# Mixing the block steps of two matrix quads in a Trainium2 encoder kernel

## The chip, the cores and the metric

The kernel runs on one core of a Trainium2 chip, as one launch for the whole computation. The core's engines have queues of their own: TensorE (PE in the profile, with its weight loads as PEld), VectorE (DVE), ScalarE (ACT), GpSimd (POOL) and SyncE (SP). SP's queue issues plain transfers, POOL's queue also transfers that add to what lies at their target. The metric is the time of one execution on the device in microseconds, as a median over runs.

## The reference

A trunk of two layers works on x of 512 tokens by 1024 features, in float32. Each layer adds attention with a projection, then a gated feed-forward network (FFN) of 2816 hidden columns:

```python
    for l in range(DEPTH):
        h = rms_norm(x, attn_norm_g[l])
        z = jnp.einsum('bsd,dc->bsc', h, w_in[l])
        ...
        mixed = jax.nn.sigmoid(ga) * ya + jax.nn.sigmoid(gb) * yb
        x = x + jnp.einsum('bsd,de->bse', mixed, w_out[l])
        h = rms_norm(x, ffn_norm_g[l])
        u = jax.nn.silu(jnp.einsum('bsd,df->bsf', h, w_gate[l])) * jnp.einsum('bsd,df->bsf', h, w_up[l])
        x = x + jnp.einsum('bsf,fd->bsd', u, w_down[l])
    return x
```

`rms_norm` divides by the root of the mean square of a token and multiplies by a gain for each feature.

## The kernel before

**Precision.** Each float32 matrix is split in a rounded high part and the low part that is left, and a product is the sum of three matmuls: high by high, high by low, low by high. The high part is a cast on ACT. The low part is either a subtraction on DVE, or it is made "by transfer": ACT writes minus the high part, and a transfer on POOL's queue adds the source to it.

**Quads.** The out projection and most of the FFN are done in quads: a product of two-by-two blocks in which seven block products stand for eight. A block step (`block_step`, numbers m = 1 to 7) is one of the seven and has 24 matmuls of 128x256. Its operands are blocks or sums of blocks. The weights' sums are made by `Quad` (`sums`, `high`, `low`), those of the data by `chain_seven`, both on DVE and ACT. A finished step is read out of its PSUM banks by DVE or ACT, and some results stay in the banks as the start of a later step: `seed` copies, and `plus`, a DVE operation of 128x512, adds one bank's result to the next step's. A step m7 waits for the `plus` behind m6, a step m4 for the one behind m7. In `ORDER` the steps of a quad run 1, 5, 6, 2, 7, 3, 4.

**A layer's second half.** First come the 14 block steps of the two `w_out` quads, q0 and q1 (`OUT_STEPS`: 1 and 5 of either, then the rest of q0, then the rest of q1). `add_x` adds each result to x, which lies in SBUF transposed, as eight tiles of 128 features by 512 tokens. When a pair of tiles is done, `gchunk` multiplies them by the gain and splits them, and squares them for the norm. Then 96 matmuls of 128x512 make the lead, the first 256 columns of gate and up, from data that is not yet divided by the norm's root; `evac_g` and `evac_u` multiply by the root's row on their way out of PSUM. In the midst of the lead stand the `ones` matmuls that sum the squares, the root on DVE (15 tiny operations), and four transposed products that spread it over the partitions (`rstd`). `begin_x` then writes x times gain times root to new tiles `xn`, and `chain_seven` makes the seven operands from them. The five FFN quads follow, each with seven steps of gate and seven of up; the down quad of the quad before runs between them. In quad 0 there is no down quad before it; eight products of the lead with the first 256 rows of `w_down` (steps "t", six matmuls of 128x512 each) stand behind the sixth step and those after it, one behind each in layer 0 and two in layer 1. Quad 0 of gate is `first`: two wide loads on SP bring its weights, and a chain of its own makes the operands as soon as something is ready.

**What sets the order.** The program is recorded by a planner. Operations on weights are queued with due times (`at_pos`) on a clock that counts PE's planned work (`tick`): so many microseconds ahead of the step that needs them (the `LEAD_` and `EARLY` numbers). Operations on data are generators (`spawn`) that the planner advances whenever the modelled engine has come near. Each engine then runs its list in that order. All tiles of SBUF come from two arenas (`arena`), packed by lifetime after a dry run, so which buffer a transfer waits for depends on the whole program. Layer 0 stores x to DRAM (`away`) while its quads run and loads it back before the last down quad; layer 1 keeps x in SBUF and transposes it with PE to the output's layout (`chain_out`).

In the profile nearly all operations carry one line, L346, the helper's. So one goes by engine, operation and shape.

Of the kernel before, what the change touches and what calls it, by code (L numbers as in the profile page):

```python
# [12 lines left out]
F32 = mybir.dt.float32  # L13
# [215 lines left out]
def trunk(ctx: ExitStack, tc: tile.TileContext, a: dict, out: bass.AP, lay: Layout):  # L229
# [208 lines left out]
    def spawn(gen, first=False):  # L438
        chains.insert(0 if first else len(chains), [gen, Need()])
# [55 lines left out]
    MOVED = (1, 2, 4)  # L495
    OUT_EARLY = (6.0, 3.0)
# [32 lines left out]

    DORDER = (1, 5, 6, 3, 7, 4, 2)  # L530
# [29 lines left out]
    OUT_STEPS = [(q, m) for q in range(2) for m in ORDER[:2]] + [(q, m) for q in range(2) for m in ORDER[2:]]  # L560
# [10 lines left out]
    def plan_ffn(l):  # L571
# [3 lines left out]
        down = a["w_down"][l]  # L575
        for step in ffn_steps(l):
            if step[0] == "m":
                _, q, w, m = step
                if m == ORDER[0]:
                    t = total[0]  # L580
# [4 lines left out]
                quads[l, q, w].due(m, total[0] - early)  # L585
                early = max(0.0, early - 1.2)
                total[0] += 24 * 0.12
            elif step[0] == "D":
                _, q, m = step
                if m == DORDER[0]:  # L590
                    f0 = 256 + 512 * q
                    srcs = [down[f0 + 256 * h : f0 + 256 * h + 256] for h in range(2)]
                    early = LEAD_LAST if q == QUADS - 1 else 0.0
                    quads[l, q, "w_down"] = Quad(srcs, total[0] - early, False, turned_quad(l, q))
                quads[l, q, "w_down"].due(m, total[0] - early)
# [75 lines left out]
    class Quad:  # L671
# [3 lines left out]
        def __init__(self, srcs, t, first, turn=False):  # L675
            self.srcs = [x.rearrange("(k p) n -> p k n", p=P) for x in srcs]
            self.first, self.turn = first, turn
            self.shape = [self.srcs[0].shape[1], self.srcs[0].shape[2] // 2]
# [21 lines left out]
        def due(self, m, t):  # L700
            if self.first:
                at_pos(t - LEAD_PREP, lambda: done.add((self, m)))
            else:
                needs = {1: [(1, 1)], 2: [(1, 2)], 3: [(1, 2)], 4: [(2, 2)], 5: [(2, 1), (2, 2)]}.get(m, [])
                lead = LEAD_PREP + (LEAD_MOVE if m in MOVED else LEAD_SUMS)
                for i, x in enumerate(needs):
                    at_pos(t - lead - LEAD_BLOCK - 2.0 * (len(needs) - i - 1), lambda x=x: self.fetch(x))
                if m in MOVED:
                    at_pos(t - lead, lambda: (self.high(m), self.low(m)))
                else:  # L710
                    at_pos(t - lead, lambda: self.sums(m))
                    at_pos(t - LEAD_PREP, lambda: self.high(m))
                    at_pos(t - LEAD_PREP + 1.8, lambda: self.low(m))

        def chain(self):


            for m in ORDER:
# [41 lines left out]
        def low(self, m):  # L760
            src, h = self.parts[m]
            lo = buf(self.shape, F32R)
            if m not in (1, 2) if self.first else m in MOVED:
# [115 lines left out]
    xp = [buf([2, S]) for _ in range(KD // 2)]  # L879
    xT = [xp[k // 2][:, k % 2] for k in range(KD)]  # L880
    away = [dp_.tile([P, 2, S], F32, tag=f"away{i}", name=f"away{i}") for i in range(KD // 2)]

    def new_x(i):
        xp[i] = buf([2, S])
        xT[2 * i : 2 * i + 2] = xp[i][:, 0], xp[i][:, 1]
# [472 lines left out]
    def layer(l):  # L1358
# [227 lines left out]
        def chain_seven(tag, parts, tiles, begin):  # L1586
# [7 lines left out]
            def low(m):  # L1594
                src, h = parts[m]
                yield Need("dve", [h], backlog=XLOG)
                lo = buf([4, 256], F32R)
                V.tensor_tensor(lo, src, h.bitcast(F32), ALU.subtract)
# [76 lines left out]
        def chain_turn():  # L1675
            yield Need(keys=[f"{key}m0"])
            for i in range(KD // 2):
                old = xT[2 * i : 2 * i + 2]
                new_x(i)
                for j in range(2):  # L1680
                    yield Need("act", [old[j]])
                    A.copy(by_columns(xT[2 * i + j]), held(old[j]))
            done.add("turned")

        spawn(chain_seven("m", ms, mt, begin_m))
# [32 lines left out]
        def add_x(q, i, t, src, sign):  # L1718
            at = 2 * q + i
            x = xp[at][:, :, 256 * t : 256 * t + 256]  # L1720
# [9 lines left out]
        for q, m in OUT_STEPS:  # L1730
# [27 lines left out]
        xn = []  # L1758

        def begin_x(h):  # L1760
            if h == 0:
                yield Need(keys=[f"rows{nrm.i}"])
                xn.extend(buf([4, S]) for _ in range(2))
# [6 lines left out]
        spawn(chain_seven("x", xs, xn, begin_x), first=True)  # L1770
# [11 lines left out]
        def evac_u(j, ps):  # L1782
            t = act()
            u[j] = act(F32R), act(F32R)
            yield Need("dve", [ps])
            V.tensor_tensor(t, ps, nrm.rows, ALU.mult)
# [257 lines left out]
```

## Time and profile before

| | |
|---|---|
| runs (three) | 1369.6, 1372.53, 1374.24 us, median 1372.53 us |
| the profiled execution | 1367.72 us, span 1365.9 us |
| granted clock of TensorE, mean | 0.999 |
| DVE, ACT, POOL busy | 77%, 64%, 23% of the span |
| DMA | 241.10 MB, mean 177 GB/s |
| first out step, lead, gate quad 0 of layer 0 | at 301.06, 342.43, 366.49 us |
| the same of layer 1 | at 973.21, 1015.46, 1039.53 us |

Times in the profile's rows count from the start of the span. A row of the timeline is a group of equal instructions that follow each other: start, length, engine, operation, count, and in brackets the idle time before them with what ended it. The last instruction of a group of matmuls ends with some 0.2 us of draining that the next group overlaps.

### The profile page before, as it was taken

How to read it: one execution, taken by the hardware profiler on the slowest of the kernel's cores; microseconds unless marked ns; L12 is line 12 of the kernel's file. 1: busy time of each engine (PE TensorE's matmuls, PEld its weight loads, DVE VectorE, ACT ScalarE, POOL GpSimd, SP SyncE). 2: the span in 40 equal slices, each digit the busy share in tenths (PEclk: the TensorE clock that was granted, in tenths of full speed). 3: DMA queues.
4: the chain of work that ended last, by engine and by line, in shares of the span. 5: the costliest groups of instructions: out<-in, count | busy, mean ns of one | idle time of the engine just before them, and what ended most of it. 6: DMA issues, size and time to landing. Idle time of an engine off the chain costs nothing.

```text
span 1365.9 us, 22021 instructions
## 1 busy us (share of the span) xinstructions
PE 1345.4 (98%) x8268; PEld 1204.3 (88%) x8268; DVE 1050.6 (77%) x1886; ACT 880.5 (64%) x1360; POOL 311.5 (23%) x335
## 2 busy tenths in 40 slices
PE   9999999999999999999999999999999999999998
PEld 7888888889889999999888888888998999899997
DVE  6876878479857697888868667784888586969888
ACT  6477667566766666757446675785766565657572
POOL 5542222321211101011253422322112111111110
PEclk9999999999999999999999999999999999999999
DMA  9997898988787769588989978879779668485883
GB/s 230 201 165 138 148 162 161 199 187 216 164 207 184 164 162 255 106 231 190 221 156 181 162 143 162 156 139 225 160 185 180 150 165 213 113 223 137 228 192 99
DMA packets 194859, 241.10 MB, mean 177 GB/s; under 512 B 27056, under 2 KB 156512, under 8 KB 194752
## 3 DMA queue, kind: packets, MB, share of 16 engines
q0 software_dynamic: 104384, 149.93, 58.1%
q1 hardware_dynamic: 89872, 89.08, 22.2%
q8 instruction: 65, 1.06, 0.3%
q10 hardware_dynamic: 496, 0.67, 0.2%
q14 instruction: 42, 0.34, 0.1%
HBM read 174.63 MB, written 4.19 MB: 131 GB/s over the span
## 4 chain that ended last, share of the span: by engine, by line
PE 72%; DVE 12%; DMA 6%; ACT 6%; issue 4%; SPq 0%; POOL 0%; ACTq 0%; DVEq 0%; POOLq 0%
PE banks L346 72%; DVE arena L346 11%; ACT arena L346 5%; DMA arena<-in_w_gate 4%; DMA arena<-in_w_up 1%; DMA arena<-in_x 1%; ACT L346 0%; SPq L346 0%; DVE banks L346 0%; ACT banks L346 0%; POOL arena L346 0%; ACT warm L346 0%; ACTq L346 0%; DVEq L346 0%; ACT sm L346 0%
## 5 line engine op out<-in xcount | busy, mean ns | idle before, releaser
L346 PE MATMUL banks<-arena 128*128 128x256 f32 (+1 forms) x7694 | 1311.2, 330 | 13.1 <-DVE arena L346 6.1
L346 PEld LDWEIGHTS banks<-arena 128*128 128x128 f32 x7694 | 1140.1, 190 | 142.4 <-ACT arena L346 8.8
L346 ACT CAST arena<-arena 128x1024 fp32r<-128x1024 f32 (+2 forms) x387 | 338.4, 903 | 176.8 <-DVE arena L346 158.2
L346 ACT ACTIVATE arena<-arena 128x1024 fp32r<-128x1024 f32 (+2 forms) x304 | 265.3, 892 | 64.5 <-DMA arena<-in_w_in 21.8
L346 DVE TENSOR_TENSOR arena<-arena,arena 128x1024 fp32r<-128x1024 f32 (+2 forms) x282 | 272.6, 978 | 35.4 <-ACT arena L346 33.4
L346 DVE TENSOR_TENSOR arena<-arena 128x1024 f32<-128x1024 f32 (+4 forms) x280 | 247.6, 897 | 22.5 <-DMA arena<-in_w_gate 18.9
L346 POOL DMA_DIRECT2D arena<-in_w_in x163 | 162.2, 1393 | 311.5 <-ACT arena L346 304.2
L346 POOL DMA_DIRECT2D arena<-arena x106 | 94.2, 888 | 579.7 <-ACT arena L346 347.5
L346 DVE TENSOR_TENSOR arena<-banks,arena 128x512 f32<-128x512 f32 (+4 forms) x234 | 155.5, 669 | 55.5 <-PE banks L346 28.0
L346 DVE TENSOR_TENSOR arena<-arena,banks 128x512 f32<-128x512 f32 (+1 forms) x201 | 135.3, 681 | 73.7 <-PE banks L346 73.6
L346 ACT COPY arena<-banks 128x512 f32<-128x512 f32 (+1 forms) x110 | 63.9, 585 | 72.3 <-PE banks L346 71.0
L346 ACT CAST arena<-banks 128x512 fp32r<-128x512 f32 (+2 forms) x116 | 64.4, 555 | 63.5 <-PE banks L346 62.4
L346 ACT ACTIVATE arena<-arena,negm 128x256 f32<-128x256 f32 (+1 forms) x128 | 68.2, 533 | 18.6 <-DVE negm L346 16.4
L346 PE MATMUL banks<-cst,arena 128*128 128x128 f32 x504 | 76.9, 274 | 1.9 <-DMA arena<-in_x 1.7
L346 PEld LDWEIGHTS banks<-cst,arena 128*128 128x128 f32 x504 | 61.5, 141 | 11.7 <-DMA arena<-in_x 2.3
L346 DVE CUSTOM_DVE_ANT_0 arena<-banks,cst,nsnk 128x256 f32<-128x256 f32 (+1 forms) x64 | 34.5, 548 | 34.1 <-PE banks L346 33.5
L346 DVE CUSTOM_DVE_ANT_0 arena<-banks,arena 128x256 f32<-128x256 f32 x64 | 26.4, 421 | 21.1 <-PE banks L346 20.8
L346 ACT ACTIVATE arena<-banks 128x512 f32<-128x512 f32 x30 | 18.0, 599 | 31.6 <-PE banks L346 31.6
L346 DVE SCALAR_TENSOR_TENSOR arena<-arena 128x512 f32<-128x512 f32 (+2 forms) x44 | 32.1, 731 | 0.6
L346 DVE TENSOR_TENSOR banks<-banks,arena 128x512 f32<-128x512 f32 x24 | 16.7, 696 | 18.4 <-PE banks L346 18.4
L346 DVE TENSOR_SCALAR arena<-arena,sm 128x256 f32<-128x256 f32 (+1 forms) x88 | 29.7, 389 | 1.1
L346 POOL DMA_DIRECT2D arena<-in_w_proj_b x16 | 17.5, 1289 | 47.7 <-ACT arena L346 47.7
(70 smaller groups left out, 351.9 us busy)
## 6 DMA issues: line engine op xcount, KB each, us to landing
arena<-arena POOLq DMA_DIRECT2D x106, 512.0 KB, 7.3
arena<-in_w_in POOLq DMA_DIRECT2D x99, 512.0 KB, 7.2
arena<-in_w_up SPq DMA_DIRECT2D x40, 512.0 KB
arena<-in_w_down SPq DMA_DIRECT2D x40, 512.0 KB
arena<-in_w_gate SPq DMA_DIRECT2D x36, 512.0 KB
arena<-in_w_in POOLq DMA_DIRECT2D x64, 256.0 KB, 6.6
arena<-in_w_proj_a POOLq DMA_DIRECT2D x16, 512.0 KB, 7.7
arena<-in_w_proj_b POOLq DMA_DIRECT2D x16, 512.0 KB, 7.4
```

The source lines that it names most:

```text
L346: f(*args, **kw)
```

## The change

The order of the 14 steps becomes `MIXED`, a table of (quad, m), for the two `w_out` quads and for gate and up of FFN quad 0, whose steps ran one matrix after the other before. The eight leading down products follow all 14 steps. Gate's quad 0 no longer is `first`: its blocks are fetched one by one and its operands have due times, 12 us early. For `w_out` the low part of m7 is now made by transfer too, and all its due times move ahead. `begin_x` scales x in place. So both layers store x to `away`, and layer 1 loads it again (`back`) at the seventh and eighth step of quad 0; the output's transposes may begin with the eleventh step instead of the third. `evac_g` and `evac_u` first copy the bank to SBUF on ACT, and DVE multiplies there. `chain_seven` makes the operand of m2 ahead of that of m6.

On PE in layer 0, before (the rows are matmuls by shape; the 336 are the 14 out steps, then the lead with `ones` and `rstd`, then quad 0 with its down products):

```order
L346 MATMUL banks<-arena_72 128x256 x336
L346 MATMUL banks<-arena_72 128x512 x45
L346 MATMUL banks<-ones,arena_71 128x1 x4
L346 MATMUL banks<-arena_72 128x512 x18
L346 MATMUL banks<-cst,rstd_3321 128x128 x4
L346 MATMUL banks<-arena_72 128x512 x33
L346 MATMUL banks<-arena_72 128x256 x144
L346 MATMUL banks<-arena_72 128x512 x6
L346 MATMUL banks<-arena_72 128x256 x24
```

and in the changed kernel:

```order
L346 MATMUL banks<-arena_72 128x256 x336
L346 MATMUL banks<-arena_72 128x512 x30
L346 MATMUL banks<-ones,arena_71 128x1 x4
L346 MATMUL banks<-arena_72 128x512 x18
L346 MATMUL banks<-cst,rstd_3302 128x128 x4
L346 MATMUL banks<-arena_72 128x512 x48
L346 MATMUL banks<-arena_72 128x256 x336
L346 MATMUL banks<-arena_72 128x512 x48
```

The `ones` stand 15 matmuls earlier in the lead, and the down products stand in one piece behind 336 matmuls instead of in pieces of six behind the sixth step and those after it.

On DVE at gate's quad 0 in layer 0. In both kernels a copy of the spread root (COPY, 128x512), four `begin_x` scalings (SCALAR_TENSOR_TENSOR with `vec2T`, 128x512) and a sum of 128x1024 stand ahead. Before, from the next row on to `plus` for gate's m7, which is the last row (the 1024-wide rows, also written 4x256, are sums, and with two sources low parts; 512-wide ones with `banks` first among the sources read PSUM):

```order
L346 TENSOR_TENSOR arena0_71<-arena0_71 128x4x256
L346 TENSOR_TENSOR arena1_72<-arena0_71,arena1_72 128x1024 x2
L346 SCALAR_TENSOR_TENSOR arena0_71<-arena0_71,vec2T_78 128x512 x4
L346 SCALAR_TENSOR_TENSOR arena0_71<-arena0_71 128x1024
L346 TENSOR_TENSOR arena0_71<-banks_73,arena0_71 128x512 x2
L346 TENSOR_TENSOR arena1_72<-arena0_71,arena1_72 128x1024 x2
L346 TENSOR_TENSOR arena0_71<-arena0_71 128x4x256
L346 TENSOR_TENSOR arena0_71<-banks_73,arena0_71 128x512
L346 TENSOR_TENSOR arena0_71<-arena0_71 128x512
L346 TENSOR_TENSOR arena1_72<-arena0_71,arena1_72 128x1024 x2
L346 SCALAR_TENSOR_TENSOR arena0_71<-arena0_71 128x1024
L346 TENSOR_TENSOR banks_73<-banks_73,arena0_71 128x512
```

In the changed kernel, up to the same `plus`; between the sum of 128x1024 named above and these rows stand two low parts, four scalings, and a subtraction, a sum and a low part of 128x1024 (of gate's and up's weights or of x):

```order
L346 TENSOR_TENSOR arena0_71<-arena0_71 128x1024
L346 TENSOR_TENSOR arena1_72<-arena0_71,arena1_72 128x1024 x2
L346 TENSOR_TENSOR arena0_71<-arena0_71 128x1024
L346 TENSOR_TENSOR arena0_71<-arena0_71 128x512 x3
L346 TENSOR_TENSOR arena1_72<-arena0_71,arena1_72 128x1024 x2
L346 TENSOR_TENSOR arena0_71<-arena0_71 128x4x256
L346 TENSOR_TENSOR arena0_71<-arena0_71 128x1024
L346 TENSOR_TENSOR arena1_72<-arena0_71,arena1_72 128x1024
L346 TENSOR_TENSOR arena0_71<-arena0_71 128x512
L346 TENSOR_TENSOR arena1_72<-arena0_71,arena1_72 128x1024 x2
L346 SCALAR_TENSOR_TENSOR arena0_71<-arena0_71 128x1024
L346 TENSOR_TENSOR banks_73<-banks_73,arena0_71 128x512
```

From the copy to `plus` there are 18 rows' worth of 1024-wide operations now, eleven before, and the lead's multiplications (128x512) no longer read `banks`.

On SP in layer 1, the difference (`-` before, `+` after):

```order
 L346 DMA arena_71<-in_w_gate 128x4x256
-L346 DMA arena_71<-in_w_gate 128x4x512 x2
+L346 DMA away_126<-arena_71 128x1024
+L346 DMA arena_71<-in_w_gate 128x4x256 x2
+L346 DMA away_127<-arena_71 128x1024
+L346 DMA arena_71<-in_w_gate 128x4x256 x2
+L346 DMA away_128<-arena_71 128x1024
 L346 DMA arena_71<-in_w_gate 128x4x256
+L346 DMA away_129<-arena_71 128x1024
 L346 DMA arena_71<-in_w_up 128x4x256 x4
+L346 DMA arena_71<-away_126 128x1024
+L346 DMA arena_71<-away_127 128x1024
```

The stores of x stand between gate's blocks, and the loads of it behind the blocks of up.

The core of the diff:

```diff
@@ spawn
-        chains.insert(0 if first else len(chains), [gen, Need()])
+        chains.insert(0 if first else len(chains), [gen, next(gen)])
@@ due times
-    MOVED = (1, 2, 4)
-    OUT_EARLY = (6.0, 3.0)
+    FIRST_MOVED = (5, 6, 7, 3, 4)
+    OUT_MOVED = (1, 2, 4, 7)
+    OUT_EARLY = (8.0, 6.0)
+    FIRST_EARLY = {"w_gate": 12.0, "w_up": 0.0}
...
+    MIXED = (
+        (0, 1), (0, 5), (1, 1), (1, 5), (0, 2), (0, 6), (1, 2),
+        (0, 7), (0, 3), (1, 6), (0, 4), (1, 7), (1, 3), (1, 4),
+    )
@@ ffn_steps
+            if not q:
+                steps += [("m", q, ("w_gate", "w_up")[i], m) for i, m in MIXED]
+                steps += [("t", *x) for x in np.ndindex(2, NB)]
+                continue
             ms = [("m", q, w, m) for w in ("w_gate", "w_up") for m in ORDER]
-            if q:
-                ds = [("D", q - 1, m) for m in DORDER]
-            else:
-                ds = [("t", *x) for x in np.ndindex(2, NB)]
+            ds = [("D", q - 1, m) for m in DORDER]
             for i, m in enumerate(ms):
                 steps.append(m)
-                for _ in range(i % 2 if q else (i >= 5) * (1 + last)):
-                    if ds:
-                        steps.append(ds.pop(0))
+                if i % 2:
+                    steps.append(ds.pop(0))
@@ plan_out
-            quads[l, q, "w_out"] = Quad(srcs, 0.0, False)
-        for q, m in OUT_STEPS:
+            quads[l, q, "w_out"] = Quad(srcs, 0.0, False, moved=OUT_MOVED)
+        for q, m in MIXED:
@@ plan_ffn
-                    early = 18.0 if q == 0 and w == "w_gate" else 0.0
+                    early[w] = FIRST_EARLY[w] if q == 0 else 0.0
...
-                    quads[l, q, w] = Quad(srcs, t - early, early > 0.0)
+                    quads[l, q, w] = Quad(srcs, total[0] - early[w], False)
@@ chain_seven
+            V.tensor_tensor(n1, b11, b12, ALU.subtract)
             yield from high(1, b11)
-            V.tensor_tensor(n1, b11, b12, ALU.subtract)
...
+            yield from high(2, b21)
+            yield from low(2)
             yield from high(6, n2)
             yield from low(6)
-            yield from high(2, b21)
-            yield from low(2)
@@ add_x
-                if l < DEPTH - 1:
-                    soon(lambda: Q.dma_start(away[at], xp[at]), 1.0)
+                soon(lambda x=pair(at): Q.dma_start(away[at], x), 1.0)
@@ begin_x
-                    xn[h][:, i], xT[4 * h + i], gain(nrm.i, 4 * h + i), nrm.rows, ALU.mult, ALU.mult
+                    xT[4 * h + i], xT[4 * h + i], gain(nrm.i, 4 * h + i), nrm.rows, ALU.mult, ALU.mult
@@ evac_g (evac_u alike)
-            yield Need("dve", [ps])
-            V.tensor_tensor(t, ps, nrm.rows, ALU.mult)
+            A.copy(t, ps)
+            yield Need("dve", [t])
+            V.tensor_tensor(t, t, nrm.rows, ALU.mult)
@@ the lead
-                        spawn((evac_u if n // 2 else evac_g)(n % 2, o))
+                        soon(lambda n=n, o=o: spawn((evac_u if n // 2 else evac_g)(n % 2, o)))
@@ the layer's FFN steps
-                if i == 2:
+                if last and i in (6, 7):
+                    back(i - 6)
+                if i == 10:
                     done.add("x_out")
```

`back(h)` takes a new tile of four features' blocks and loads two of the four stored pairs into it.

More of the change, by code (lines that the diff above doesn't have):

```diff
@@ L592, in plan_ffn @@
                     srcs = [down[f0 + 256 * h : f0 + 256 * h + 256] for h in range(2)]
-                    early = LEAD_LAST if q == QUADS - 1 else 0.0
-                    quads[l, q, "w_down"] = Quad(srcs, total[0] - early, False, turned_quad(l, q))
-                quads[l, q, "w_down"].due(m, total[0] - early)
+                    early["w_down"] = LEAD_LAST if q == QUADS - 1 else 0.0
+                    quads[l, q, "w_down"] = Quad(srcs, total[0] - early["w_down"], False, turned_quad(l, q))
+                quads[l, q, "w_down"].due(m, total[0] - early["w_down"])
                 at_pos(total[0] - LEAD_V, lambda key=("go", l, q, m): done.add(key))
@@ L704, in due @@
                 needs = {1: [(1, 1)], 2: [(1, 2)], 3: [(1, 2)], 4: [(2, 2)], 5: [(2, 1), (2, 2)]}.get(m, [])
-                lead = LEAD_PREP + (LEAD_MOVE if m in MOVED else LEAD_SUMS)
+                moved = m in self.moved
+                lead = LEAD_PREP + (LEAD_MOVE if moved else 0.0) + (0.0 if m in (1, 2, 4) else LEAD_SUMS)
                 for i, x in enumerate(needs):
                     at_pos(t - lead - LEAD_BLOCK - 2.0 * (len(needs) - i - 1), lambda x=x: self.fetch(x))
-                if m in MOVED:
-                    at_pos(t - lead, lambda: (self.high(m), self.low(m)))
-                else:
+                if m not in (1, 2, 4):
                     at_pos(t - lead, lambda: self.sums(m))
-                    at_pos(t - LEAD_PREP, lambda: self.high(m))
-                    at_pos(t - LEAD_PREP + 1.8, lambda: self.low(m))
+                    lead -= LEAD_SUMS
+                at_pos(t - lead, lambda: self.high(m))
+                at_pos(t - lead + (0.0 if moved else 1.8), lambda: self.low(m))
         def chain(self):
-            for m in ORDER:
+            for m in (m for i, m in MIXED if not i):
                 yield Need(keys=[(self, m)], backlog=XLOG)
@@ L762, in low @@
             lo = buf(self.shape, F32R)
-            if m not in (1, 2) if self.first else m in MOVED:
+            if m in self.moved:
                 low_by_transfer(lo, src, h)
@@ L877, in gain, with new_x, pair, back @@
         return vec2T[:, 16 + c : 17 + c] if norm % 2 else vecT[:, c : c + 1]
-    xp = [buf([2, S]) for _ in range(KD // 2)]
-    xT = [xp[k // 2][:, k % 2] for k in range(KD)]
+    xq = [buf([4, S]) for _ in range(2)]
+    xT = [xq[k // 4][:, k % 4] for k in range(KD)]
     away = [dp_.tile([P, 2, S], F32, tag=f"away{i}", name=f"away{i}") for i in range(KD // 2)]
-    def new_x(i):
-        xp[i] = buf([2, S])
-        xT[2 * i : 2 * i + 2] = xp[i][:, 0], xp[i][:, 1]
+    def new_x(h):
+        xq[h] = buf([4, S])
+        xT[4 * h : 4 * h + 4] = [xq[h][:, i] for i in range(4)]
+    def pair(i):
+        return xq[i // 2][:, 2 * (i % 2) : 2 * (i % 2) + 2]
+    def back(h):
+        new_x(h)
+        for i in (2 * h, 2 * h + 1):
+            Q.dma_start(pair(i), away[i])
     nsnk = cp.tile([P, DEPTH, 8], F32, tag="nsnk", name="nsnk")
@@ L1584, in layer, with chain_seven @@
             yield from gates(zb)
-        def chain_seven(tag, parts, tiles, begin):
+        def chain_seven(tag, parts, tiles, begin, moved):
             def high(m, src):
@@ L1676, in chain_turn @@
             yield Need(keys=[f"{key}m0"])
[L1677 to L1682, printed above, removed]
+            for h in range(2):
+                old = xT[4 * h : 4 * h + 4]
+                new_x(h)
+                for t, o in zip(xT[4 * h : 4 * h + 4], old):
+                    yield Need("act", [o])
+                    A.copy(by_columns(t), held(o))
             done.add("turned")
-        spawn(chain_seven("m", ms, mt, begin_m))
+        spawn(chain_seven("m", ms, mt, begin_m, ()))
         if l == DEPTH - 1:
@@ L1719, in add_x @@
             at = 2 * q + i
-            x = xp[at][:, :, 256 * t : 256 * t + 256]
+            x = pair(at)[:, :, 256 * t : 256 * t + 256]
             op = ALU.add if sign > 0 else ALU.subtract
@@ L1726, in add_x @@
                     spawn(nrm.gchunk(2 * at + j))
[L1727 to L1730 removed]
+                soon(lambda x=pair(at): Q.dma_start(away[at], x), 1.0)
+        for q, m in MIXED:
             yield f"m{l}{m}"
@@ L1784, in evac_u @@
             u[j] = act(F32R), act(F32R)
-            yield Need("dve", [ps])
-            V.tensor_tensor(t, ps, nrm.rows, ALU.mult)
+            A.copy(t, ps)
+            yield Need("dve", [t])
+            V.tensor_tensor(t, t, nrm.rows, ALU.mult)
             done.add(f"{key}up{j}")
@@ L2001, in layer @@
                     norms[2 * l + 2] = Norm(2 * l + 2)
-                    for i in range(KD // 2):
-                        new_x(i)
-                        Q.dma_start(xp[i], away[i])
+                    back(0)
+                    back(1)
                     for k in reversed(range(KD)):
```

21 lines of the change are left out of this document (11 added, 10 removed).

## The prediction, made before the changed kernel was run

> **What bounds the kernel now.** I read the page's busy times, then what TensorE (PE) waits for, then busy time by stretch, and last the rows of the stretches that the change rewrites.
>
> ```profile
> PE 1345.4 (98%) x8268; PEld 1204.3 (88%) x8268; DVE 1050.6 (77%) x1886; ACT 880.5 (64%) x1360; POOL 311.5 (23%) x335
> ```
> ```profile
> PE banks L346 <- DVE arena L346: 7.2, 11, 1.2
> PE banks L346 <- DVE banks L346: 3.8, 2, 1.9
> ```
>
> PE is busy for 98% of the span, and the change removes no matmul. So all that can be won is idle PE time, or PE time at a reduced clock, and all that can be lost is new idle time. The second fence (engine, what it waits for, total, times, longest) says that PE waits mostly for VectorE (DVE). Where? These are the stretches that the change rewrites, in layer 0 and then layer 1: the out projection, the lead columns of gate and up, and quad 0 of gate and up with the leading down products (bounds, length, busy time of PE, its weight loads, DVE, ACT and POOL, then granted clock, DMA share, GB/s).
>
> ```profile
> 301.06:342.43 41.37, 40.79 (x338) 40.41 (x337) 38.61 (x43) 27.20 (x34) 5.42 (x6) 1.00 0.75 200
> 342.43:366.49 24.06, 23.47 (x110) 19.22 (x109) 20.65 (x38) 16.89 (x21) 5.48 (x5) 1.00 0.78 160
> 366.49:405.00 38.51, 35.75 (x269) 34.07 (x268) 25.31 (x29) 27.42 (x35) 7.51 (x7) 1.00 0.87 206
> 973.21:1015.46 42.25, 40.78 (x338) 40.41 (x336) 38.61 (x43) 27.20 (x34) 5.42 (x6) 1.00 0.68 171
> 1015.46:1039.53 24.07, 23.48 (x111) 19.23 (x110) 20.66 (x38) 16.89 (x21) 6.26 (x6) 1.00 0.75 141
> 1039.53:1078.00 38.47, 35.71 (x256) 33.94 (x255) 25.23 (x30) 25.58 (x35) 6.76 (x6) 0.96 0.78 173
> ```
>
> In the out projection DVE is busy 38.61 of 41.37 us, so PE runs close behind DVE there. The single waits, in PE's timeline of layer 0 and then layer 1 (start, length, count, idle before and who ended it):
>
> ```profile
> 324.52 14.63 PE L346 MATMUL banks<-arena 128*128 128x256 f32 x120 [0.27 <-DVE arena L346]
> 353.40 1.05 PE L346 MATMUL banks<-ones,arena 128*128 128x1 f32 x8 [0.59 <-DVE arena L346]
> 373.61 5.90 PE L346 MATMUL banks<-arena 128*128 128x256 f32 x47 [0.88 <-DVE arena L346]
> 381.38 43.79 PE L346 MATMUL banks<-arena 128*128 128x256 f32 x319 [1.88 <-DVE banks L346]
> ...
> 1012.49 13.36 PE L346 MATMUL banks<-arena 128*128 128x256 f32 x69 [1.19 <-DVE arena L346]
> 1026.44 1.05 PE L346 MATMUL banks<-ones,arena 128*128 128x1 f32 x8 [0.59 <-DVE arena L346]
> 1046.64 5.89 PE L346 MATMUL banks<-arena 128*128 128x256 f32 x47 [0.88 <-DVE arena L346]
> 1054.41 3.13 PE L346 MATMUL banks<-arena 128*128 128x256 f32 x18 [1.88 <-DVE banks L346]
> ```
>
> The first row gives the beat: 120 matmuls of 256 columns in 14.63 us less some 0.2 for the last to drain, so 0.120 us each and 2.88 us for a block step of 24. Fourteen out steps should take 14 x 2.88 = 40.32 us. They take 41.37 and 42.25, so 1.05 us are lost in layer 0 and 1.93 in layer 1; both places are a step m4 right behind m7 of its own quad. The ones matmuls of the norm lose 0.59 in either layer. Gate starts at 366.49; its third step, m6, should start 5.76 later and starts at 373.61: 1.36 lost. The fifth, m7, should start 5.76 after that and starts at 381.38: 2.01 lost. Layer 1 repeats both (1.35 and 2.01) and pays once more:
>
> ```profile
> 1052.29:1055.70 3.41, 1.53 (x14) 1.35 (x13) 3.38 (x6) 3.10 (x4) 0.21 (x1) 1.00 1.06 353
> 1055.70:1059.12 3.42, 3.42 (x19) 3.42 (x18) 1.69 (x2) 1.01 (x2) 0.69 (x1) 0.50 1.03 234
> 1062.53:1065.94 3.41, 3.41 (x29) 3.29 (x28) 0.00 (x0) 2.60 (x6) 1.20 (x1) 1.00 0.41 45
> 379.86:383.27 3.41, 1.89 (x16) 1.92 (x17) 3.41 (x5) 2.10 (x3) 0.88 (x1) 1.00 1.19 302
> ```
>
> Behind a stretch of 3.41 us in which PE worked only 1.53, the clock is granted at 0.50 for the next 3.42 us, which costs half of it, 1.71 us. In layer 0 the same wait lies across two such stretches, the fuller of which still worked 1.89, and the clock stays.
> Loss before: layer 0 1.05 + 0.59 + 1.36 + 2.01 = 5.0; layer 1 1.93 + 0.59 + 1.35 + 2.01 + 1.71 = 7.6; together 12.6 us.
>
> Further losses lie in layer 1's FFN, where steps are not reordered, but where fetches and buffers move (PE twice, then DVE in layer 1 and at the same place of layer 0, then the chain of waits):
>
> ```profile
> 1163.63 12.78 PE L346 MATMUL banks<-arena 128*128 128x256 f32 x88 [1.01 <-DVE arena L346]
> 1177.06 3.11 PE L346 MATMUL banks<-arena 128*128 128x512 f32 x18 [0.66 <-ACT arena L346]
> ...
> 1225.87 12.78 PE L346 MATMUL banks<-arena 128*128 128x256 f32 x88 [1.01 <-DVE arena L346]
> 1239.31 2.87 PE L346 MATMUL banks<-arena 128*128 128x512 f32 x16 [0.66 <-ACT arena L346]
> ```
> ```profile
> 1157.86 1.23 DVE L346 TENSOR_TENSOR arena<-arena 128x1024 f32<-128x1024 f32 x1 [6.69 <-DMA arena<-in_w_gate]
> 477.48 1.23 DVE L346 TENSOR_TENSOR arena<-arena 128x1024 f32<-128x1024 f32 x1 [4.29 <-DMA arena<-in_w_gate]
> ```
> ```profile
> 1137.17 20.61 DMA arena<-in_w_gate
> ```
>
> DVE sums two blocks of the next gate quad; the later block takes 20.61 us to land, DVE stands 6.69 us, and 4 to 6 us later PE stands 1.01 + 0.66, with seams of 0.2 to 0.3 us beside them, so about 2 us for each of two quads: 3.9 us. In layer 0 DVE stands 2.4 us less (6.69 - 4.29), and PE does not stand.
>
> **The change, part by part.**
>
> *Mixed steps of the out projection.* No work is added; q0's m7 and m4 get steps of q1 between them, q1's m4 gets m3 ahead of it. DVE's `plus` for an m4 then has a whole step, 2.88 us, more than before, against lateness of 0.3 to 1.2 us: the 1.05 and 1.93 go. What is late next is m7 of q0, now the eighth step, 7 x 2.88 = 20.2 us in. Behind the last evacuation of the stage before, which I put at 1 to 2 us in, the order has 14 DVE rows 1024 wide (1.13 us each, below) and one 512 wide (0.60) ahead of its `plus`: 17.4 to 18.4, and 0.7 for itself, 18.1 to 19.1; casts on ACT between these rows can use up the 1.1 to 2.1 in hand. I take 0.1, bounds 0 and 0.7 (one `plus` more). The low part of w_out's m7 moves from DVE to ACT and a POOL transfer: one 1.2 us row less on DVE, one more on ACT, which is busy 27.20 of 41.37.
>
> *Ones matmuls of the norm.* They stand behind 30 instead of 45 lead matmuls of 512 columns. The rows: lead matmuls on PE, the last `add_x` on DVE, and ACT's table load, a 1024-wide and a 512-wide operation.
>
> ```profile
> 354.32 4.37 PE L346 MATMUL banks<-arena 128*128 128x512 f32 x18
> ...
> 344.30 0.68 DVE L346 TENSOR_TENSOR arena<-arena,banks 128x512 f32<-128x512 f32 x1
> ...
> 343.16 1.28 ACT L346 ACT_TABLE_LOAD   x1
> 344.56 1.05 ACT L346 ACTIVATE arena<-arena 128x1024 fp32r<-128x1024 f32 x1
> 350.25 0.62 ACT L346 ACTIVATE arena<-arena 128x512 f32<-128x512 f32 x1
> ```
>
> 18 matmuls in 4.37 us less the drain are 0.23 each, so PE asks 15 x 0.23 = 3.4 us earlier, 30 x 0.23 = 6.8 after the lead's start. On DVE eight rows follow the last `add_x` before, five now (3.7 us); the three gone are 1024 wide, 3 x 1.13 = 3.4 us. If `add_x` ends as before, at 344.98 or lead + 2.5, DVE alone is ready at lead + 6.2. But ACT feeds these rows: from lead + 0.7 (343.16) the table and a short first use, 1.5, two 1024-wide operations, 2.0, and four 512-wide ones, 2.4, make lead + 6.6, and two DVE rows behind it, 1.3, make 7.9. I take this, 1.1 us late, bounds 0 and 1.2; it is 0.5 more than before.
>
> *Scaled in place, gate and up mixed, down products behind.* The DVE rows between the factor's copy and `plus` for gate's m7:
>
> ```profile
> 359.16 0.69 DVE L346 COPY arena<-banks 128x512 f32<-128x512 f32 x1 [0.60 <-PE banks L346]
> 359.89 2.74 DVE L346 SCALAR_TENSOR_TENSOR arena<-arena,vec2T 128x512 f32<-128x512 f32 x4
> 362.66 2.36 DVE L346 TENSOR_TENSOR arena<-arena 128x1024 f32<-128x1024 f32 x2
> 380.54 0.69 DVE L346 TENSOR_TENSOR banks<-banks,arena 128x512 f32<-128x512 f32 x1
> ```
>
> Start to start these give 0.68 us for a 512-wide scaling, 1.13 for a 1024-wide row, 0.60 for a 512-wide one. Before, `plus` came 21.4 us after the copy. Now the order has there 8 scalings (5.4), 18 rows 1024 wide (20.3) and 4 of 512 (2.4), and the copy's 0.7: it starts 28.8 and ends 29.5 us after the copy. PE asks later as well: the copy hangs on the ones matmuls, gate comes 10.7 us after the copy (13.1 from ones to gate before, 3.4 more now, less the 5.8 from ones to copy), and m7 is the eighth step, 7 x 2.88 = 20.2: 30.9. That is 1.4 us in hand. But DVE also waits for ACT in this stretch of before:
>
> ```profile
> DVE arena L346 <- ACT arena L346: 6.8, 4, 3.0
> ```
>
> 6.8 us in four waits, the longest 3.0. About 1.8 us of such waits in the 28.8 makes m7 late by 0.4, which I take; bounds 0 (none) and 1.6 (one of 3.0). Gate's m6 is now sixth, 14.4 us behind gate's start, its low part ready at about copy + 21 against copy + 25: the 1.36 goes. With no wait near 1.5 us in one 3.41 us stretch the clock stays, and the 1.71 goes.
>
> *The evacuation copies.* Eight ACT copies from PSUM:
>
> ```profile
> L346 ACT COPY arena<-banks 128x512 f32<-128x512 f32 x78 | 45.2, 585 | 58.2 <-PE banks L346 57.5
> ```
>
> 4 x 0.585 = 2.3 us on ACT per layer, in stretches where ACT has 7 and 11 us free. DVE's multiplication from SBUF takes a 512-wide row as before. Hidden; if ACT falls behind, the `plus` above waits for it, within the bounds given. The eight leading down products, 48 matmuls of 512 columns, no longer cover DVE between the steps; the tally above is already made without them.
>
> *Stores and reloads of x.* Layer 1 gains four stores and four loads of 512 KB on SP's queue. At the 353 GB/s of the fullest row above one takes 1.5 us, 12 us in all, in 63 us of stretches with DMA shares of 0.75 and 0.78, so some 15 us free. They are issued ahead of the w_up blocks and of the next quad's blocks respectively. The loads are issued at the seventh and eighth of the 14 steps; the transposes of x that need them begin at the end of the twelfth, over 4 x 2.88 = 11.5 us later. I take 0; bounds 0 and 3 (two transfers of 1.5 late on a block that PE waits for). Gate's wide loads become blocks: same bytes.
>
> *Later fetches.* In the built program the buffers of layer 1's late pairs are freed by instructions that stand 4 to 6 us earlier than before; the pair that took 20.61 us needs to be only some 2 us earlier to fit, as layer 0 shows. In layer 0 one pair's second fetch is freed 4.3 us later, behind an emptier queue. I take 3.0 of the 3.9 as gone; bounds +2 (layer 0 catches the wait) and -3.9.
>
> **Sum.** Left behind per layer 0.1 + 1.1 + 0.4 = 1.6. Layer 0: 5.0 - 1.6 = 3.4; layer 1: 7.6 - 1.6 = 6.0; FFN 3.0: together 12.4 us. The profiled execution took 1367.72 us, 4.8 below the median of the three runs, 1372.53; from the median the sum gives 1360.1, and I say 1360.5 for seams of 0.2 us that no row prices.
>
> [...] The row: PE idle for 1.88 us in one piece was followed by 3.42 us at half clock in layer 1, not in layer 0. [...] Of the stretch from 1062.53 this row was more than half:
>
> ```profile
> 1063.50 1.91 PE L346 MATMUL banks<-cst,arena 128*128 128x128 f32 x16
> ```
>
> [...]
>
> **Rivals.**
> 1. *The FFN wait stays*, since the DMA queues are as full as before whoever frees the buffers. Then 9.4 us, or 7.4 if layer 0 catches it too: 1363 to 1365. For it: landing times of 20.61 us on a queue shared with POOL's accumulating transfers, which remain.
> 2. *The stall moves instead of going.* DVE's work in out projection and gate is unchanged, 38.61 of 41.37 us there, and without down products between steps gate's PE beat is 2.88 us a step. If ones lose 1.2, m7 of either quad its upper bounds 0.7 and 1.6, and the later steps as much again as these in each layer, 2 x 7 = 14 us stand against 12.6: within 0.3%, 1370 to 1374. Against it: 30.9 against 29.5 above.
> 3. *Slower: fetch pairs late in every quad.* Four quads per layer follow quad 0. If the repacked buffers delay the pair in each by 1.2 us more than layer 0's slack, each costs the 2 us of the rows above: 8 x 2 = 16 against 9.4 won, 1372.5 + 6.6 = 1379. It decides from five late quads on. Against it: only two of eight stood before.
> 4. *The clock falls in a new place*, at 1.5 to 1.9 us of idle time in one stretch: +1.71 for each layer, 1362 to 1364.
>
> **Chances.** Less than 0.3%, 4.1 us, cannot be told from no change here. Forecast 0.47 (1356 to 1362.5), rival 1 0.24, rival 4 0.08, rival 2 0.13, rival 3 and its like 0.08. Faster: 0.47 + 0.24 + 0.08 and a little of rival 2, 0.81; same 0.12; slower 0.07. The range runs from 1355 (all 12.6 and 3.9 gone and 1 us of the runs' own spread) to 1370.
>
> **What would show it.** Right: no wait longer than 0.7 us ahead of an out step; ones with about 1 us; gate's sixth step without a wait and the eighth with under 1.6; clock 1.00 in every stretch of layer 1; no 1.01 wait behind the gate fetches of layer 1's FFN. Wrong: DVE rows of the norm waiting for ACT, `plus` of gate's m7 more than 1.6 us late, up steps waiting for the POOL transfers of their low parts, or DVE idle for DMA at the start of FFN quads in both layers.

## The result and the profile after

| | before | changed |
|---|---|---|
| median, first comparison (5 runs each) | 1369.6 us | 1360.58 us (1358.05 to 1361.46) |
| ratio | | 0.9924, 95% interval 0.9898 to 0.9951 |
| median, beside the later experiments | 1366.62 us | 1360.28 us |
| ratio | | 0.9955, 95% interval 0.9943 to 0.9968 |
| span of the profiled execution | 1365.9 us | 1359.7 us, in the repeat 1356.7 us |

The change makes the kernel faster, by 4 to 14 us if one takes both intervals. The time is that of the forecast. The sum behind it was too large: in layer 1 a wait stands that it put at 0.1 us, and the clock falls behind it. How that fits together is shown below.

What PE waits for in the changed kernel (engine, what for, total, times, longest), from the same view as before:

```profile
PE banks L346 <- DVE banks L346: 5.5, 4, 4.3
PE banks L346 <- DVE arena L346: 1.8, 4, 0.7
```

The 7.2 us of waits for DVE's sums and low parts are 1.8 now. The waits for a `plus` (`DVE banks`) have grown from 3.8 to 5.5, and one of them alone is 4.3 us long. PE's timeline, layer 0 and then layer 1, shows where (start, length, count, idle time before):

```profile
323.64 27.24 PE L346 MATMUL banks<-arena 128*128 128x256 f32 x198 [0.28 <-DVE banks L346]
351.58 1.05 PE L346 MATMUL banks<-ones,arena 128*128 128x1 f32 x8 [0.70 <-DVE arena L346]
388.81 17.75 PE L346 MATMUL banks<-arena 128*128 128x256 f32 x146 [0.45 <-DVE banks L346]
...
997.14 28.70 PE L346 MATMUL banks<-arena 128*128 128x256 f32 x198 [4.34 <-DVE banks L346]
1026.54 1.05 PE L346 MATMUL banks<-ones,arena 128*128 128x1 f32 x8 [0.70 <-DVE arena L346]
1063.77 14.27 PE L346 MATMUL banks<-arena 128*128 128x256 f32 x117 [0.45 <-DVE banks L346]
```

In layer 0 the three places that the prediction named are left: m7 of the first out quad (0.28), `ones` (0.70), gate's m7 (0.45). Beside them stands only a wait of 0.22 us for an accumulating transfer in up's last step. Gate's m6 and the out steps m4 run without a wait. Layer 1 is the same but for 4.34 us ahead of m7 of the first out quad, and behind it the clock is lower:

```profile
993.45:996.87 3.42, 0.00 (x0) 0.00 (x0) 2.90 (x4) 3.39 (x4) 0.00 (x0) 1.00 0.61 115
996.87:1000.28 3.41, 3.14 (x14) 3.14 (x15) 1.93 (x3) 1.24 (x2) 1.63 (x2) 0.53 0.51 94
1077.90:1083.10 5.20, 5.20 (x50) 5.20 (x48) 2.11 (x4) 4.27 (x8) 0.70 (x1) 1.00 0.98 214
```

(bounds, length, busy time of PE, its loads, DVE, ACT, POOL, then clock, DMA share, GB/s.) Behind 3.42 us in which PE did nothing, the clock is granted at 0.53 for 3.41 us, some 1.6 us lost. The last row holds the 32 transposes of x, closer together than before: the clock stays at 1.00.

Who is late? DVE's timeline in layer 1, with the same sum in layer 0 as its last row, and then the chain of waits:

```profile
965.54 0.68 DVE L346 TENSOR_TENSOR arena<-arena,banks 128x512 f32<-128x512 f32 x1
971.31 1.22 DVE L346 TENSOR_TENSOR arena<-arena 128x1024 f32<-128x1024 f32 x1 [5.09 <-DMA arena<-in_w_out]
972.45 0.68 DVE L346 TENSOR_TENSOR arena<-arena,banks 128x512 f32<-128x512 f32 x1
...
295.77 1.22 DVE L346 TENSOR_TENSOR arena<-arena 128x1024 f32<-128x1024 f32 x1
```
```profile
952.42 18.76 DMA arena<-in_w_out
996.48 0.62 DVE banks L346
```

DVE's sum for m5 of the second w_out quad needs a block that takes 18.76 us to land. DVE stands 5.09 us in front of it, with evacuations of the stage before queued behind, and from there on it runs behind until the `plus` at 996.4 makes PE wait. In layer 0 the same sum (295.77) meets no such wait. In the kernel before, layer 1 fetches its w_out blocks in the same bunch, from 937.9 us on, and by the completion events of the trace the sixth lands 16.0 us after its issue. But there the due times are 2 and 3 us later, and DVE waits for none of these blocks. So late blocks are not new; what is new is a sum that stands in front of one.

In the FFN of layer 1 the four waits of 0.66 to 1.01 us are gone; what is left there is

```profile
PE banks L346 <- DVE arena L346: 0.2, 1, 0.2
```

### The profile page after: what moved, and what is told of

The parts are those of the page before. It is cut to its first block, busy times and chain, and to the rows that moved or that the text cites. A ratio compares the mean times of both kernels' runs of the same rounds, so it can differ in the third digit from the quotient of the medians.

```text
span 1359.7 us, 22061 instructions
## 1 busy us (share of the span) xinstructions
PE 1344.8 (99%) x8268; PEld 1206.1 (89%) x8268; DVE 1052.0 (77%) x1886; ACT 884.5 (65%) x1368; POOL 308.0 (23%) x335
## 4 chain that ended last, share of the span: by engine, by line
PE 80%; DVE 9%; DMA 4%; ACT 4%; issue 3%; POOL 0%; SPq 0%; DVEq 0%; ACTq 0%; POOLq 0%
PE banks L346 80%; DVE arena L346 8%; ACT arena L346 3%; DMA arena<-in_w_out 1%; DMA arena<-in_w_down 1%; DMA arena<-in_w_in 1%; DMA arena<-arena 1%; DMA arena<-in_w_gate 1%; DVE sm L346 0%; ACT L346 0%; DMA arena<-in_x 0%; DVE banks L346 0%; POOL arena L346 0%; SPq L346 0%; ACT warm L346 0%
## 5 line engine op out<-in xcount | busy, mean ns | idle before, releaser
L346 DVE TENSOR_TENSOR arena<-arena 128x1024 f32<-128x1024 f32 (+4 forms) x288 | 252.0, 890 | 7.9 <-DMA arena<-in_w_out 5.1
L346 POOL DMA_DIRECT2D arena<-arena x106 | 91.1, 859 | 601.1 <-ACT arena L346 389.0
L346 DVE TENSOR_TENSOR arena<-banks,arena 128x512 f32<-128x512 f32 (+4 forms) x226 | 150.2, 668 | 58.4 <-PE banks L346 31.0
L346 ACT COPY arena<-banks 128x512 f32<-128x512 f32 (+1 forms) x118 | 68.5, 584 | 75.6 <-PE banks L346 74.1
```

The source lines that it names most:

```text
L346: f(*args, **kw)
```

## The experiments

Every variant was timed in rounds beside the kernel before, on one chip per group. The ratios are to the kernel before of the same group. The changed kernel stands in one of these groups alone, as `after_again`; against the other groups it is compared by the ratios or across chips.

| label | median us | before us | ratio (95% interval) |
|---|---|---|---|
| out_only | 1368.82 | 1367.37 | 1.0007 (0.9992 to 1.0022) |
| gate_only | 1366.11 | 1367.37 | 0.9985 (0.9967 to 1.0002) |
| sums_late | 1360.37 | 1367.37 | 0.9937 (0.9918 to 0.9957) |
| pairs_ahead | 1362.7 | 1367.37 | 0.9956 (0.9934 to 0.9978) |
| after_again | 1360.28 | 1366.62 | 0.9955 (0.9943 to 0.9968) |
| out_ahead | 1363.15 | 1366.62 | 0.9974 (0.9965 to 0.9982) |
| both_ahead | 1361.14 | 1366.62 | 0.9961 (0.9949 to 0.9973) |
| no_gate_copy | 1358.97 | 1366.62 | 0.9945 (0.9932 to 0.9958) |
| all_out_ahead | 1363.06 | 1367.45 | 0.9965 (0.9951 to 0.9979) |
| three_moves | 1360.83 | 1367.45 | 0.9953 (0.9940 to 0.9967) |
| sums_pairs | 1360.84 | 1367.45 | 0.9950 (0.9936 to 0.9963) |
| less_dma | 1354.6 | 1370.23 | 0.9888 (0.9861 to 0.9915) |

**The two halves of the change.** `out_only` is the kernel before with these lines of the change (the core of its edit)

```diff
-    OUT_STEPS = [(q, m) for q in range(2) for m in ORDER[:2]] + [(q, m) for q in range(2) for m in ORDER[2:]]
+    OUT_STEPS = MIXED
-    OUT_EARLY = (6.0, 3.0)
+    OUT_EARLY = (8.0, 6.0)
+    OUT_MOVED = (1, 2, 4, 7)
```

> The kernel before with only the out projection mixed (its order, its due times, m7's low part by transfer); gate, up, x and the rest as before. Theory 1: the new wait of 4.3 us in layer 1's out projection belongs to this part, since DVE's sum for m5 of the second w_out quad now stands ahead of the last evacuations and waits for a late block. Then layer 0 gains some 0.5 us, layer 1 wins 1.9 and loses 4.5 and 1.7 (clock): 2 to 5 us slower than before, 1372 to 1375, or 1368 to 1371 if the FFN waits of 3.9 us go with the new buffers. Theory 2: the wait comes from the wider tiles of x, which free their room later: it is absent here, 1366 to 1368.

`gate_only` is the changed kernel with these lines as they were.

> The changed kernel with the out projection in its old order and with its old due times. Theory 1: the gate waits of 3.4 us in either layer and the half clock of 1.7 are gone, the out waits of 1.05 and 1.9 stay, the wait for w_out is absent: 8.4 us less than before, 12 with the FFN waits gone, 1357 to 1361. Theory 2 (x tiles): the wait for w_out is here, 1363 to 1367.

PE's timeline of `out_only` in layer 1 (out m7, `ones`, gate m6 and m7), and of `gate_only` in layer 0 (`ones`, gate m7):

```profile
998.99 33.14 PE L346 MATMUL banks<-arena 128*128 128x256 f32 x213 [4.47 <-DVE banks L346]
1032.43 1.05 PE L346 MATMUL banks<-ones,arena 128*128 128x1 f32 x8 [0.30 <-DVE arena L346]
1052.60 5.90 PE L346 MATMUL banks<-arena 128*128 128x256 f32 x47 [0.88 <-DVE arena L346]
1060.37 2.39 PE L346 MATMUL banks<-arena 128*128 128x256 f32 x18 [1.87 <-DVE banks L346]
```
```profile
353.57 1.16 PE L346 MATMUL banks<-ones,arena 128*128 128x1 f32 x8 [3.72 <-DVE arena L346]
392.46 20.61 PE L346 MATMUL banks<-arena 128*128 128x256 f32 x169 [0.46 <-DVE banks L346]
```

The new wait is 4.47 us in `out_only`, with the old tiles of x, so it belongs to the mixed out projection with its due times: theory 1. The clock from 995 to 1003 us is 0.68 in the mean. The time, 1368.82, is that of theory 1 with most of the FFN waits gone, and 1.1 of their 3.9 us are left. The old gate waits, 0.88 and 1.87, stand there untouched. In `gate_only` they are gone, and what is left at gate's m7 is 0.46, as in the changed kernel. But its time missed the 1357 to 1361 of theory 1: with the out steps in their old order `ones` wait 3.72 us in layer 0, where DVE waits 4.69 us for ACT and ACT 2.9 us for a block of up's lead columns, which none of the theories had. Behind the 3.72 us the clock is 0.63 in the mean from 353.5 to 357 us. In layer 1 `ones` wait 1.96 us; the mean clock of the whole execution is 0.997, before 0.999. Neither half alone is worth much: the halves are not independent, since fetches, buffers and DVE's order are planned for both together.

**The repeat, and the gate copies.**

> The changed kernel once more, beside the others on one chip. If its wait of 4.3 us in layer 1's out projection is fixed by the program's order and buffers, the profile shows it again within 0.3 us, with the half clock or without it by where the 3.41 us windows fall; median 1359 to 1362. If it came from one execution's transfers, it is absent or under 2 us.

> The changed kernel with the lead's gate evacuated by DVE straight from PSUM, without the two ACT copies per layer. If the copies are hidden and only spare PSUM room, the time is that of the changed kernel, within 1.5 us. If they are what keeps DVE's queue from standing behind the lead, gate's eighth step comes 1 us or more later in either layer: 2 us or more slower.

```diff
 def evac_g
-            A.copy(t, ps)
-            yield Need("dve", [t])
-            V.tensor_tensor(t, t, nrm.rows, ALU.mult)
+            yield Need("dve", [ps])
+            V.tensor_tensor(t, ps, nrm.rows, ALU.mult)
```

The row of layer 1's out m7 in the repeat, then in `no_gate_copy`:

```profile
994.10 28.73 PE L346 MATMUL banks<-arena 128*128 128x256 f32 x198 [3.33 <-DVE banks L346]
```
```profile
994.60 28.73 PE L346 MATMUL banks<-arena 128*128 128x256 f32 x198 [3.07 <-DVE banks L346]
```

So the wait is the program's, 3.3 to 4.3 us by the execution; not "within 0.3". By these rows the clock falls there too: the 198 matmuls take 28.7 us, as in the first profile, against 27.2 in layer 0 at a clock of 1.00. Without the gate copies the time is that of the changed kernel (the intervals overlap), so as work they cost nothing and buy no time. Its median is below the changed kernel's, but not separable from it.

**Moving what waits.** `sums_late` changes one due time, `pairs_ahead` another (in the kernel before):

```diff
 sums_late: w_out, second quad
+            quads[l, q, "w_out"].held = {5: 5.0} if q else {}
...
                 if m not in (1, 2, 4):
+                    lead -= self.held.get(m, 0.0)
                     at_pos(t - lead, lambda: self.sums(m))
 pairs_ahead: gate quads 1 to 4, m5
+                    quads[l, q, w].pair_ahead = q > 0 and w == "w_gate"
...
+                ahead = 6.0 if m == 5 and self.pair_ahead else 0.0
...
-                    at_pos(t - lead - LEAD_BLOCK - 2.0 * (len(needs) - i - 1), lambda x=x: self.fetch(x))
+                    at_pos(t - lead - LEAD_BLOCK - ahead - 2.0 * (len(needs) - i - 1), lambda x=x: self.fetch(x))
```

> The changed kernel with one due time moved: the sum for m5 of the second w_out quad (and what follows from it) 5 us later, behind two evacuations on DVE instead of ahead of them; its blocks are fetched at the same due time. Theory 1 (DVE's queue stands behind that sum): the wait of 4.3 us and the half clock behind it go, 6 us less than the changed kernel, 1353 to 1356. Rival: the block is late for the step itself, so PE waits at m5 of the second quad instead: 1358 to 1361.

> The kernel before with one thing moved: the two blocks behind m5 of every gate quad but the first are fetched 6 us earlier by their due times. If the FFN waits of layer 1 come from these blocks landing late, they go: 3 to 4 us less than before, 1365 to 1367. If the transfers wait for buffers or for the full queues, whatever their due times: within 1 us of before, about 1369.

`pairs_ahead` did what theory 1 said and a little more, 0.9956. PE's waits in the FFN of layer 1 are 0.2 us in all:

```profile
PE banks L346 <- DVE arena L346: 0.2, 1, 0.2
```

So the 3.9 us of FFN waits come from pairs that land late, and a due time cures them. The mixed order is not needed for that. In the changed kernel they went as the late blocks of the two quads landed sooner, at 1149.9 and 1203.5 us instead of 1157.8 and 1220.0; which of its moves brought that was not tried. In `gate_only`, `sums_late` and `out_ahead` about 2 us of them were back in one quad.

In `sums_late` DVE no longer waits for w_out, and PE's wait is

```profile
994.51 27.22 PE L346 MATMUL banks<-arena 128*128 128x256 f32 x198 [1.69 <-DVE banks L346]
```

1.69 instead of 4.34, with the clock at 1.00. But the time stayed at 1360.37 against 1353 to 1356 expected: waits of 1.0 and 0.65 us were back in a later FFN quad of layer 1, and in layer 0 0.83 us in up's last step and 0.93 at the leading down products were new. That the new packing of the buffers brought them is likely and not shown.

**Fetching w_out earlier.** Three kernels moved the fetches by the same kind of edit: the pair for the second quad's m5 by 10 us (`out_ahead`; `both_ahead` with the gate pairs too), or all eight blocks by 8 us (`all_out_ahead`).

> The changed kernel with the two blocks behind m5 of the second w_out quad fetched 10 us earlier by their due times, so that they stand second or third instead of near last in SP's queue. Theory 1 (that block lands late behind six others, and DVE's queue stands behind its sum): the wait of 4.3 us and the half clock go, 5 to 6 us less than the changed kernel beside it. Rival: the other blocks are late in their turn and a wait of the same size comes up at m5 of the first quad or at m6: within 1 us of it.

> As out_ahead, and the two blocks behind m5 of every gate quad but the first are fetched 6 us earlier too. If the FFN waits hang on when buffers happen to come free, this makes sure that none stands: the time of out_ahead, or 2 us per wait less than it if it has any; 1352 to 1356 and the fastest. If earlier fetches crowd out POOL's accumulating transfers, a new wait on low parts shows, 1357 to 1361.

> The changed kernel with all eight w_out blocks of either layer fetched 8 us earlier by their due times (out_ahead moved two of them ahead of the rest). In the built program they get buffers that in layer 1 come free sooner: none but one waits for an evacuation later than the copies of x. Theory 1, sharpened by out_ahead (eight blocks issued in a bunch from 937 us on, the last two land 19 us later): DVE's wait for w_out falls under 1.5 us and PE's wait in layer 1 from 3.3 to 4.3 down to 0.5 to 1.7; 3 to 5 us less than the changed kernel, 1355 to 1358. Rival: DMA is the bound there, so they land as late as before or push POOL's transfers back: within 1 us of it.

All three missed theory 1's times. In `out_ahead` DVE still waits 5.1 us for a w_out block, in `both_ahead` 3.2; PE's waits at out m7 of layer 1 are 0.78 and 2.38 us, in layer 0 1.36 and 1.98. In `all_out_ahead` the wait of layer 1 at out m7 is 0.29 us, as that theory had it, and two others stand in its place, one ahead of the out projection and one in layer 0:

```profile
965.60 31.35 PE L346 MATMUL banks<-arena 128*128 128x512 f32 x216 [2.35 <-DVE arena L346]
997.24 3.02 PE L346 MATMUL banks<-arena 128*128 128x256 f32 x23 [0.29 <-DVE banks L346]
...
324.59 25.78 PE L346 MATMUL banks<-arena 128*128 128x256 f32 x185 [2.38 <-DVE banks L346]
```

That fits the rival of `all_out_ahead`, that w_out's blocks push other transfers back: between 930 and 1010 us ACT waits 14.1 us for blocks of w_proj_a and w_proj_b, 10.3 and 11.6 in the two profiles of the changed kernel, and DVE's longest wait for ACT is 6.7 us against 3.4 and 4.2. The 185 matmuls behind the 2.38 us take 25.78 us, where 191 of the same group take 25.65 in the changed kernel, so by this estimate the clock fell there as well. Two combinations follow:

> all_out_ahead, with the sum for m5 of the second w_out quad 5 us later (sums_late) and the gate pairs 6 us earlier (pairs_ahead). If the three losses are separate, their gains add: no wait of PE over 1.7 us in out projection or FFN, 1353 to 1357, the fastest. If the new buffers bring a wait back elsewhere, 1358 to 1361.

> sums_late and pairs_ahead together, without the gate copies (which cost nothing in no_gate_copy). w_out's fetches stay as in the changed kernel. PE's wait in layer 1's out projection as in sums_late, 1.7 us, and no FFN wait: 1356 to 1359; if the FFN waits come back with other buffers, 1359 to 1361.

Neither beat the changed kernel. In `three_moves` out m7 is down to 0.9 us in layer 1, but 2.53 us of waiting for an accumulating transfer came up at the end of layer 0's up steps, and the 27 matmuls behind it take 5.53 us, where the first 27 there take 4.44 in the changed kernel. In `sums_pairs` out m7 waits 1.61 us, as expected, but 2.41 us of waiting for DVE came up ahead of the out projection.

**Is it the DMA?** The last kernel takes load off the queues and leaves the lists of PE, DVE, ACT and SP as they are. It leaves out six transfers that the result needs, so it is a probe and no kernel to use:

```diff
 w_low
-            for at, ap in src:
+            for at, ap in src if i not in range(84, 90) else ():
```

> The changed kernel without six of POOL's accumulating transfers, those of the low parts of the last six slabs of weights ahead of layer 1's out projection (so these low parts stay minus the high part, and what is computed differs). w_out's fetches keep their order, and the last one still waits for the same evacuation. Theory 1 (the DMA queues are full from 935 to 970 us, so that w_out's last blocks land 19 us after their issue): they land within 13 us, DVE does not wait for them and PE's wait in layer 1's out projection is under 1 us, as in layer 0; 3 to 6 us less than the changed kernel, 1354 to 1357. Rival: it is DVE's order and the place of its sums alone: PE still waits 3 us or more.

The stretch of layer 1 from 935 to 970 us, of the changed kernel and then of `less_dma`, and from the latter's timeline its out m7:

```profile
935.00:970.00 35.00, 35.00 (x156) 28.84 (x156) 17.53 (x23) 20.86 (x29) 8.17 (x9) 1.00 1.17 259
```
```profile
935.00:970.00 35.00, 35.00 (x156) 28.98 (x155) 21.85 (x28) 23.35 (x30) 3.45 (x4) 1.00 0.62 167
```
```profile
991.52 27.25 PE L346 MATMUL banks<-arena 128*128 128x256 f32 x198 [0.28 <-DVE banks L346]
```

Without six of POOL's accumulating transfers the DMA share falls from 1.17 to 0.62 (the share adds up the packets' times, so it can pass 1). By the completion events of the trace the block that took 18.8 us lands 3.7 us after its issue, and PE waits 0.28 us, as in layer 0. The time is 1354.6 us, 5.7 below the changed kernel on another chip, or 9 by the two ratios; the wait and the clock make 5.7 in the first profile and 4.8 in the repeat. DVE's list is the same in both kernels, so the cause is shown: the load on the DMA queues while w_out's blocks are to land, with DVE's sum in front of one. It is not the six transfers alone, for the four fetches of w_proj between them on POOL go out by 928 us now instead of 942, and that lightens the stretch too. ACT's waits for w_proj are gone as well, but from 960 to 1010 us DVE waits 1.3 us for ACT in either kernel, so the wait does not come by way of ACT.

The share alone does not tell the two layers apart. Layer 0 has 1.11 to 1.23 from 258 to 278 us, and there five of the eight blocks are issued from 257 on, 46 us ahead of the out steps; the last two, issued at 283, land after 6.5 and 9.4 us. Layer 1 issues all eight between 937.5 and 952.9, the first 35 us ahead, since that one waits for a buffer that copies on ACT hold until 937.4. That the bunching alone would do is not shown, since the variants that spread the fetches shifted other buffers too.

## Why the prediction was right, and where it was not

The forecast was 1360.5 us against a shown median of 1372.53, that is 12 us less. The measured time is 1360.58, but the kernel before came out at 1366.6 to 1370.2 in all later groups: the three runs shown were high samples. The drop is 6 to 9 us, and the sum of 12.4 too large.

- *Out projection, layer 0.* Predicted 0.1 us left at m7 of the first quad, bounds 0 to 0.7: 0.28.
- *Out projection, layer 1.* The step that failed. The prediction put the last evacuation of the stage before at 1 to 2 us behind the first out step, for both layers, with ACT as the only other cause of waits. The first out steps are at 303.05 and 972.48 us. In layer 0 DVE ended that evacuation 1.8 us in, in layer 1 6.0, since DVE had stood 5.09 us in front of the late block. From there to the end of `plus` it took 18.7 and 18.6 us, so the rest of the price was the same in both layers, some 1.6 over the 17.1 of the rows. The change moves DVE's sums ahead (`OUT_EARLY`), and the prediction did not ask whether their blocks would be there, though the row of 20.61 us for a gate block lay in the same text. The term of 0.1, bound 0.7, came out at 4.34 and 3.33, with the clock at about 6 and 5 us. So two of the signs that it named for being right failed in layer 1: no wait over 0.7 us ahead of an out step, and a clock of 1.00.
- *Ones.* 1.1 predicted, 0.70 measured; the bounds held.
- *Gate and up mixed, scaled in place.* 0.4 predicted at m7, 0.45 measured in both layers; the 1.36 at m6 is gone. The step went nearly as worked out: PE asked 31.0 us after the copy (30.9 predicted), and `plus` ended 31.4 after it (29.5 and 1.8 of waits for ACT); one such wait of 1.1 us stands there, and the rest lies in the rows.
- *Clock.* The loss at gate is gone, and half clock came back in the out projection (0.53 from 996.87 to 1000.28 us). Rival 4 named the price, 1.71, and not the place.
- *Stores, reloads, copies.* Hidden, as taken: no wait for x appears, and `no_gate_copy` times the same.
- *FFN.* 3.0 of 3.9 predicted as gone, all but 0.2 measured. `pairs_ahead` confirms the cause; why the change removes it is open.

In idle time: layer 0 fell from 5.0 to 0.28 + 0.70 + 0.45 = 1.4, plus 0.2 in up's last step (3.4 won, 3.4 predicted); layer 1 from 7.6 to 4.34 + 0.70 + 0.45 + 1.6 = 7.1 (0.5 won, 6.0 predicted); FFN 3.7 won. Together 7.6; the spans differ by 6.2. Executions also differ ahead of the out steps: layer 0's begin at 303.05 us in the first profile and at 300.11 in the repeat, 301.06 before. So it is partly luck that the number is so close: one error, a wait that was not seen, was offset by a reference that was high by some 3 to 6 us.

On the clock behind waits: the half clock that the prediction read behind 1.88 us of waiting stood here behind 4.34, as 0.53 over the 3.41 us that followed 3.42 without work. In `gate_only` 0.63 in the mean from 353.5 to 357 us followed a wait of 3.72 us. The transposes of x cost no clock where rows show them: 16 of them filled 1.91 of the 3.41 us from 1062.53 us on before, and 32 stand in the 5.20 us from 1077.90 us on in the changed kernel, with 1.00 in both stretches.

## What to carry to other kernels

When operations are moved ahead, ask for each operand when its transfer lands and how full the queues are by then; DVE in front of a late block holds back everything behind it in its list, here 5 us on DVE and 4.3 on PE some 26 us later. Price each layer or repetition from its own rows, since what runs beside it can differ. And where buffers are packed anew with every edit, a gain or loss of a few microseconds far from the edit may belong to the packing: test it by a due time of its own, as `pairs_ahead` did.

## What the runs showed of the hardware

A 512 KB block issued on SP's queue took 18.8 us to land at a DMA share of 1.17, and 3.7 us when six accumulating transfers of 512 KB of POOL's queue were absent and four fetches went out earlier (share 0.62). In the five variants that fetched blocks earlier other waits came up, and their medians were 0.6 to 2.9 us above the changed kernel's 1360.28.

Behind waits of PE the clock fell in some places and not in others, and the length of the wait alone did not tell them apart. Before, the 1.88 us at gate's m7 stand in both layers. In layer 1 PE was busy 1.53 of the 3.41 us from 1052.29 us on, and the next 3.42 us had 0.50; in layer 0 it was busy 1.89 of the 3.41 us from 379.86 us on, and the next 3.41 us had 1.00. In the changed kernel PE was busy 0.00 of the 3.41 us from 993.64 us on, and the next 3.41 us had 0.50. In `sums_late`, with a wait of 1.69 us, the clock was 1.00 from 992 to 996 us, and the 198 matmuls behind it took 27.22 us, as in layer 0 of the changed kernel (27.24). In `all_out_ahead` 2.35 us of waiting cost no clock that shows: the 216 matmuls behind them took 31.35 us, and 217 without such a wait 31.42 in `less_dma`. The 2.38 us of the same run were followed by the 185 matmuls that took longer than 191 in the changed kernel.
